# Row maxima at 0.615 instead of 0.57 steps per group of three products, in the second layer of a diffusion backbone

## The chip, the core and the metric

The kernel runs on one core of a Trainium2 chip. TensorE (PE) multiplies; VectorE (DVE), ScalarE (ACT) and GpSimd (POOL) do the rest, and SyncE (SP) issues most loads. Each engine works through its own instructions in order, and semaphores tie them together. The metric is the device time of one execution in microseconds, the median of several.

## The reference

Two layers run over 2048 latent tokens of width 1024 on a grid of 32 rows by 64 columns, with 256 context tokens ahead of them. The second layer (layer 1 in the code) is neighbourhood attention with 16 heads of 64. Cut to what matters:

```python
q, k, v, z = jnp.split(jnp.dot(h, w_in), 4, axis=-1)      # 1024 columns each, latent and context tokens
q, k = rms_norm(q, q_gain), rms_norm(k, k_gain)            # per head
s_lat = einsum(q_row, k_window) * scale + rpb              # 8 grid rows, 16 of 64 columns left by a mask
s_ctx = einsum(q_row, k_ctx) * scale                       # 256 context tokens
p = softmax(concat([s_lat, s_ctx]))
o = p_lat @ v_window + p_ctx @ v_ctx
y = jnp.dot(o * silu(z), w_out)
```

## The kernel before

Everything is float32, and products are made of three passes of rounded parts (`hi*hi + hi*lo + lo*hi`); such a group of three matmuls of 512 columns for one slice of 128 of the inner dimension is one **step**. Tokens go in tiles of 128: `NT` = 18 tiles, the first `NCT` = 2 of them context.

Layer 1 has three stages. `odd_qk` makes queries and keys and writes them to DRAM (`Q1`, `K1`, `K1t`). `odd_vz`, the stage of the change, does two things at a time:

- **The projections** of values and gates, PE's main stream. A cell (t, j) is tile t times the 512 columns j: 4 and 5 are the values, 6 and 7 the gates. A cell has 8 steps (lines L131 to L133, bank `gm`). Values go over ACT to DRAM on POOL's queue (`V1`, `V1c` for context); gates pass a tanh, a product on DVE (L1639) and four transposes (L1642, tile `tp`) to DRAM. There are 65 cells: tiles 15 to 17 first, then from 14 down to 0; the last four are the values of tiles 1 and 0. `reload` brings each tile's hidden state from DRAM (L394) and splits it into `hhi` and `hlo` (L399).
- **The row maxima**, `maxes()`. For each of 16 heads and 16 blocks of 128 queries, a "row" takes the largest score that the softmax will subtract later: a product with the 256 context keys (L1689; its maxima for two rows are one reduction, L1691) and one with a window of latent keys (L1696), to whose pieces DVE adds the bias table and takes the maximum (L1702). The queries come by a small load per four rows (`mq`, L1683) which ACT sorts into `mz`; the tables come per head (`mtab`, L1673), and POOL adds the window's mask to them (L1674, L1675). PE and DVE pass the scores through five PSUM banks `mx`. At a head's end the maxima are transposed (L1658) and go to `M1` in DRAM.

`weave` joins the two: after each projection step it adds `ratio` to what is due and issues that many rows. With `head` = 32, rows begin when four cells are done. A row may fall behind its step by `lag` = 15; past that the projections are held until it is issued, and once the rows have all been asked for, the hold tightens by the same ratio:

```python
n = len(done) - lag - 1 + int(over)
if n >= 0:
    es.enter_context(self.tc.issue_after(done[min(n, len(done) - 1)].ins))
```

The order on each engine within these bounds is laid out when the program is built, by a scheduler with a time model of its own.

`odd_attention` follows. Its loads run in one chain on SP (`load`, L113), in this order: queries of head 1 (`q11`, `q21` and their maxima from `M1`), a group of keys (`kt`), values (`ov`), two bias tables (`tab`), context keys (`kc`), queries of head 0, more keys, the context values, the mask (`maskk`), and then the next pair of heads. The first scores are those with the context keys (L1786, L1787, tile `st`). The scores with latent keys wait in `st` until DVE adds the table (L1945), to which POOL has added the mask (L1783). These tiles take over memory of the stage before: the query tile `q11` lies where the row maxima had their keys `mk`, and `maskk` lies where the last projection weights are.

Of the kernel before, what the change touches and what calls it, by code (L numbers as in the profile page):

```python
# [61 lines left out]
def rect(kind, g, c):  # L62

    (r, nr), (k, nk) = reach(kind, 0, g), reach(kind, 1, c)
    while nr * nk < 256:
        k, nk = (k, nk + 1) if k == 0 else (k - 1, nk + 1)
    return (r, nr), (k, nk)


def even(a, n):  # L70

    b = a // 2 * 2
    return b, (a + n + 1) // 2 * 2 - b, a - b


def pieces(kind, ax, g, a, n):

    blocks, u = BLOCKS[kind][ax], AXES[ax][2]
    out = []
    for p in range(n):  # L80
        i = blocks.index((g, a + p) if (g, a + p) in blocks else (1, a + p - u * (g - 1)))
        if out and out[-1][1] + out[-1][2] == i:
            out[-1][2] += 1
        else:
            out.append([p, i, 1])
    return out


class Kern:
# [1523 lines left out]
    def odd_vz(self, ws, win, hT):  # L1613
# [4 lines left out]
        with ExitStack() as es:  # L1618
# [37 lines left out]
            def row(h, mc):  # L1656
                pt = self.tl(pp, [P, 512], "mx", bufs=5)
                nc.tensor.transpose(pt[:16, :P], mc[:], self.ident[:])  # L1658
                r = self.tl(mp, [P, P], "mr", F32R, bufs=1)
                self.act(r[:16], pt[:16, :P], AF.Copy, scale=-1.0)  # L1660
                for g in range(4):
                    nc.gpsimd.dma_start(self.M1[h, g * 512 : g * 512 + 512].rearrange("(a c b) -> c a b", a=8, c=4),
                                        r[4 * g : 4 * g + 4].rearrange("c (a b) -> c a b", a=8).bitcast(F32))

            def maxes():
                for h in range(16):
                    j, b = h // 2, (h % 2) * 64
                    with self.tc.issue_after(self.wload.ins):
                        if b == 0:
                            k = self.tl(mp, [P, T], "mk", F32R, bufs=2)  # L1670
                            nc.sync.dma_start(k[:].bitcast(F32), self.K1[j])
                        tb = self.tl(mp, [P, NR, NC], "mtab", bufs=2)
                        nc.sync.dma_start(tb[:], self.i["rpb_q"][h].rearrange("p (r c) -> p r c", r=NR))  # L1673
                    nc.gpsimd.tensor_tensor(out=tb[:], in0=tb[:], in1=mk[:, :NR].unsqueeze(2).to_broadcast([P, NR, NC]), op=ALU.add)  # L1674
                    nc.gpsimd.tensor_tensor(out=tb[:], in0=tb[:], in1=mk[:, NR:].unsqueeze(1).to_broadcast([P, NR, NC]), op=ALU.add)  # L1675
                    m = self.tl(mp, [P, 16, 5], "mm")
                    nc.vector.memset(m[:], -3e38)
                    kl = k[:, CTX:].rearrange("d (r c) -> d r c", r=32)
                    for R in range(16):
                        g, c = divmod(R, 4)  # L1680
                        if c == 0:
                            q = self.tl(mp, [P, 512], "mq", F32R, bufs=1)
                            nc.sync.dma_start(q[b : b + 64].bitcast(F32), self.Q1[0, j, b : b + 64, g * 512 : g * 512 + 512])  # L1683
                            zt = zq[h % 2][g % 2]
                            self.by_tile(zt[b : b + 64], q[b : b + 64])
                        lh = zt[:, c * P : c * P + P]
                        if c % 2 == 0:
                            pc = self.tl(pp, [P, 2, CTX], "mx", bufs=5)
                        nc.tensor.matmul(pc[:, c % 2, :], lh, k[:, :CTX], start=True, stop=True)  # L1689
                        if c % 2 == 1:  # L1690
                            nc.vector.tensor_reduce(out=m[:, R - 1 : R + 1, 0], in_=pc[:], axis=AX.X, op=ALU.max)  # L1691
                        (r0, nr), (c0, w) = rect("q", g, c)
                        ps = self.tl(pp, [P, 512], "mx", bufs=5)
                        a, n, d = even(c0, w)
                        ps = ps[:, : nr * n].rearrange("p (r c) -> p r c", r=nr)
                        mm = nc.tensor.matmul(ps, lh, kl[:, r0 : r0 + nr, a : a + n], start=True, stop=True)  # L1696
                        ps = ps[:, :, d : d + w]
                        n = 1
                        for ro, ri, rn in pieces("q", 0, g, r0, nr):
                            for co, ci, cn in pieces("q", 1, c, c0, w):  # L1700
                                s = ps[:, ro : ro + rn, co : co + cn]
                                nc.vector.tensor_tensor_reduce(out=s, in0=s, in1=tb[:, ri : ri + rn, ci : ci + cn], scale=1.0,  # L1702
                                                               scalar=-3e38, op0=ALU.add, op1=ALU.max, accum_out=m[:, R, n : n + 1])
                                n += 1
                        yield mm
                        if R == 5 and h:
                            row(*turn)
                    mc = self.tl(mp, [P, 16], "mc", bufs=1)
                    nc.vector.tensor_reduce(out=mc[:], in_=m[:], axis=AX.X, op=ALU.max)
                    turn = (h, mc)  # L1710
                row(*turn)
# [1 line left out]
            first = [NT - 3, NT - 2, NT - 1]  # L1713
            cells = self.cells(first + list(range(NT - 3))[::-1], (4, 5, 6, 7), lambda t, j: (j > 4 or t < NT - 3) and (j < 6 or t >= NCT))
            gemms = self.stream(cells, hT, cell, lambda t: self.reload(1, t))
            self.weave(gemms, maxes(), 0.57, 15, 32)


    def odd_attention(self, out, right, left, wout):
# [508 lines left out]
```

## Time and profile before

| | |
|---|---|
| median of 3 runs | 3563.59 us (3560.05 to 3564.49) |
| the profiled execution | 3565.63 us, of it 3563.9 us from first to last instruction |
| busy: PE, DVE, ACT, POOL | 97%, 68%, 41%, 35% |
| the stage of the change: first row product to last projection | 2556.3 to 2985.2 us of the span |
| from the last projection to the first score product of attention | 19.55 us without PE |
| last instruction of the span | 3563.9 us |

Most times below are positions in the span. "A <- B" in a list of waits means that A waited for B; behind it stand the total in us, the number of times and the longest. A line of a timeline has start and duration in us, the engine, the source line, the operation, the tiles it writes and reads, and in brackets the idle time before it and what ended that. SPq is SP's DMA queue as its sequencer issues it.

### The profile page before, as it was taken

What the parts mean: (1) busy time and instruction counts of PE and PEld (TensorE: products, weight loads), DVE (VectorE), ACT (ScalarE), POOL (GpSimd) and SP (SyncE); (2) the same over time, 40 slices, a digit from 0 to 9 for tenths busy, and PEclk for the clock granted to TensorE, in tenths of its full rate; (3) what the DMA queues carried; (4) which work ended last, traced back from release to release, by engine and by line L of the source; (5) the groups of instructions that cost most, each with busy time, mean ns of one, the idle gap of its engine ahead of it and who ended that gap; (6) DMA issues with size and microseconds to landing.
All of it is one profiled execution on the core that took longest, in us unless ns stands there. A gap on an engine that the chain in (4) does not pass through costs nothing. (4 is left out here: it accounts for less than half of the span.)

```text
span 3563.9 us, 54063 instructions
## 1 busy us (share of the span) xinstructions
PE 3453.2 (97%) x19460; PEld 2666.8 (75%) x19460; DVE 2431.0 (68%) x4798; ACT 1449.8 (41%) x2647; POOL 1243.9 (35%) x1400
## 2 busy tenths in 40 slices
PE   7999999999999999999999999999999997999999
PEld 6888987888896666665557878888788885556577
DVE  4677756888885777768876655444477874666875
ACT  5445542111113554546664354544322222555532
POOL 1333431111111333422211144334234443888852
PEclk9999999999999999999999999999999998999999
DMA  7555555232315242334525765445744447888684
GB/s 253 144 158 157 152 141 152 91 107 93 102 65 165 62 133 80 103 116 132 176 79 142 144 193 151 134 138 164 244 139 159 155 152 183 206 223 219 192 234 79
DMA packets 379596, 526.75 MB, mean 148 GB/s; under 512 B 34633, under 2 KB 254233, under 8 KB 372882
## 3 DMA queue, kind: packets, MB, share of 16 engines
q1 hardware_dynamic: 326450, 405.32, 39.3%
q0 software_dynamic: 29856, 82.14, 9.2%
q10 hardware_dynamic: 23024, 35.85, 3.0%
q8 instruction: 154, 2.52, 0.3%
q14 instruction: 112, 0.92, 0.1%
HBM read 344.39 MB, written 196.60 MB: 152 GB/s over the span
## 5 line engine op out<-in xcount | busy, mean ns | idle before, releaser
L699 DVE TENSOR_REDUCE mm<-mx 128x1 f32<-128x512 f32 (+1 forms) x656 | 388.3, 627 | 82.5 <-PE mx L698 75.5
L108 ACT ACTIVATE apt<-st 128x1024 f32<-128x1024 f32 (+1 forms) x296 | 300.0, 1014 | 313.2 <-PE st L1168 298.0
L1175 DVE TENSOR_TENSOR acc<-acc,apt 128x1024 f32<-128x1024 f32 x256 | 340.6, 1330 | 80.6 <-ACT apt L108 61.5
L1168 PE MATMUL st<-aq,akh 64*128 64x512 f32 x1728 | 313.9, 411 | 1.1 <-ACT apt L108 0.8
L1078 PE MATMUL av<-apt,av 128*64 128x512 f32 x1152 | 265.8, 598 | 0.0
L1945 DVE TENSOR_TENSOR opt<-st,tab 128x64 f32<-128x64 f32 (+10 forms) x576 | 144.2, 315 | 151.0 <-PE st L1787 67.6
L1826 POOL TENSOR_TENSOR oacc<-oacc,opt 128x576 f32<-128x576 f32 (+5 forms) x192 | 223.3, 1186 | 39.2 <-ACT rl L108 19.6
L698 PE MATMUL mx<-mk,mq 96*128 96x512 f32 (+1 forms) x656 | 236.0, 373 | 0.5 <-DVE mm L699 0.5
L1168 PE MATMUL st<-aq,akl 64*128 64x512 f32 (+1 forms) x1152 | 231.4, 393 | 0.0
L1702 DVE CUSTOM_DVE_ANT_1 mx<-mx,mtab 128x217 f32<-128x217 f32 (+12 forms) x576 | 183.6, 339 | 53.3 <-PE mx L1696 40.6
L108 ACT ACTIVATE u<-gm 128x352 f32<-128x352 f32 (+1 forms) x140 | 68.4, 496 | 370.9 <-PE gm L133 208.5
L1168 PEld LDWEIGHTS st<-aq,akh 64*128 64x128 f32 x1728 | 154.1, 187 | 83.6 <-ACT apt L108 28.0
L1078 PEld LDWEIGHTS av<-apt,av 128*64 128x64 f32 x1152 | 76.2, 136 | 135.3 <-issue 134.3
L108 ACT ACTIVATE opt<-opt 128x930 f32<-128x930 f32 (+8 forms) x130 | 104.5, 805 | 108.6 <-DVE opt L1945 104.2
L698 PEld LDWEIGHTS mx<-mk,mq 96*128 96x128 f32 x656 | 121.2, 188 | 12.9 <-DVE mm L699 1.6
L1168 PEld LDWEIGHTS st<-aq,akl 64*128 64x128 f32 (+1 forms) x1152 | 112.6, 186 | 24.2
L1691 DVE TENSOR_REDUCE mm<-mx 128x2 f32<-128x512 f32 x128 | 88.3, 690 | 46.1 <-PE mx L1689 45.0
L220 POOL TENSOR_TENSOR oss<-oss,mhalf 128x8 f32<-128x8 f32 x68 | 113.3, 1666 | 5.0
L131 PE MATMUL gm<-w1h,hhi 128*128 128x512 f32 x280 | 112.2, 401 | 0.0
L133 PE MATMUL gm<-w1h,hlo 128*128 128x512 f32 x280 | 110.3, 394 | 0.0
L1786 PE MATMUL st<-q,kt 128*128 128x480 f32 (+5 forms) x256 | 99.5, 391 | 11.1 <-DVE opt L1945 8.1
L132 PE MATMUL gm<-w1l,hhi 128*128 128x512 f32 x280 | 110.0, 393 | 0.0
(694 smaller groups left out, 9743.9 us busy)
## 6 DMA issues: line engine op xcount, KB each, us to landing
q<-Q SPq DMA_DIRECT2D x48, 512.0 KB
H<-x ACTq DMA_DIRECT2D x32, 512.0 KB
adaw<-ada_w SPq DMA_DIRECT2D x64, 256.0 KB
wraw<-w_od SPq DMA_DIRECT2D x64, 256.0 KB
K1t<-okt POOLq DMA_DIRECT2D x32, 512.0 KB, 10.1
kt<-K1t SPq DMA_DIRECT2D x32, 512.0 KB
x<-H SPq DMA_DIRECT2D x31, 512.0 KB
mtab<-rpb_q SPq DMA_DIRECT2D x16, 899.0 KB
```

The costliest lines, as they stand in the source:

```text
L108: return self.nc.scalar.activation(out, in_, func, **kw)
L131: self.nc.tensor.matmul(out, lh(k), rh(k), start=start and j == 0, stop=False)
L133: yield self.nc.tensor.matmul(out, ll(k), rh(k), start=False, stop=stop and j == n - 1)
L220: return g.tensor_tensor(out=out, in0=out, in1=self.mhalf[:, : shp[1]], op=ALU.pow)
L698: mm = nc.tensor.matmul(ps[:, :w], q[:A_QK, (t % 6) * P : (t % 6) * P + P], k[:A_QK, k0 : k0 + w], start=True, stop=True)
L699: nc.vector.tensor_reduce(out=m[:, t, n : n + 1], in_=ps[:, :w], axis=AX.X, op=ALU.max)
L1078: mm = nc.tensor.matmul(O[j, nb][i * 64 : i * 64 + 64, :w], V[j, kt // TT][:, kt % TT, i * 64 : i * 64 + 64], pts[:, i, :w], start=n == 0, ...
L1168: mm = nc.tensor.matmul(ps[:, o // 64, :w], k[o : o + r, kb, kq], Q[o : o + r, qb, :w], start=m == 0, stop=m == 4)
L1175: added = nc.vector.tensor_tensor(out=acc[:, :, :w], in0=a[:, :, :w], in1=pts[:, :, :w], op=ALU.add)
L1702: nc.vector.tensor_tensor_reduce(out=s, in0=s, in1=tb[:, ri : ri + rn, ci : ci + cn], scale=1.0, scalar=-3e38, op0=ALU.add, op1=ALU.max, a ...
L1826: self.psum = nc.gpsimd.tensor_tensor(out=a, in0=a, in1=pts[:, :, a0 - r0 : a1 - r0, :], op=ALU.add)
L1945: bias = nc.vector.tensor_tensor(out=pt[:, d[0], d[1]], in0=ps[:, d[0], d[1]], in1=tabs[j][i][:, ri : ri + rn, ci : ci + cn], op=ALU.add)
```

## The change

One number: `ratio` in the call that weaves the stage goes from 0.57 to 0.615. Nothing is computed differently, and no instruction is added or taken away but for how rows of the same kind stand beside each other.

```diff
             gemms = self.stream(cells, hT, cell, lambda t: self.reload(1, t))
-            self.weave(gemms, maxes(), 0.57, 15, 32)
+            self.weave(gemms, maxes(), 0.615, 15, 32)
```

Two places show what moves. The first is PE where the last head's last rows stand. Before, they stand in the first half of cell (1, 5), whose bank is `gm_4836`; one more cell follows it.

```order
L132 MATMUL gm_4836_27919<-w1l_4003_23377,hhi_4785_27603 128x512
L133 MATMUL gm_4836_27919<-w1h_4002_23376,hlo_4786_27604 128x512
L1696 MATMUL mx_4817_27787<-mk_4734_27333,mz11_4051_23653 128x384
L131 MATMUL gm_4836_27919<-w1h_4002_23376,hhi_4785_27603 128x512
L132 MATMUL gm_4836_27919<-w1l_4003_23377,hhi_4785_27603 128x512
L133 MATMUL gm_4836_27919<-w1h_4002_23376,hlo_4786_27604 128x512
L131 MATMUL gm_4836_27919<-w1h_4002_23376,hhi_4785_27603 128x512
L132 MATMUL gm_4836_27919<-w1l_4003_23377,hhi_4785_27603 128x512
L133 MATMUL gm_4836_27919<-w1h_4002_23376,hlo_4786_27604 128x512
L1696 MATMUL mx_4822_27811<-mk_4734_27333,mz11_4051_23653 128x288
```

Now they stand at the seam between cells (2, 5) and (2, 6), banks `gm_4819` and `gm_4821`:

```order
L1689 MATMUL mx_4801_27645<-mk_4719_27205,mz11_4051_23653 128x256 x2
L132 MATMUL gm_4819_27755<-w1l_4003_23377,hhi_4770_27466 128x512
L133 MATMUL gm_4819_27755<-w1h_4002_23376,hlo_4771_27467 128x512
L1696 MATMUL mx_4802_27647<-mk_4719_27205,mz11_4051_23653 128x384
L131 MATMUL gm_4821_27784<-w2h_4031_23538,hhi_4770_27466 128x512
L132 MATMUL gm_4821_27784<-w2l_4032_23539,hhi_4770_27466 128x512
L133 MATMUL gm_4821_27784<-w2h_4031_23538,hlo_4771_27467 128x512
L1696 MATMUL mx_4807_27671<-mk_4719_27205,mz11_4051_23653 128x288
```

From the last L1696 on, 12 projection steps stood behind it and 47 stand there now, with two sets of gate transposes among them. Through the middle of the stage the rows lag by 15 to 17 in both programs.

The second place is SP's queue where the last small loads of the rows meet the first loads of attention. Before:

```order
L394 DMA x_4829_27857<-H 128x1024
L1683 DMA mq_4764_27503<-Q1 64x512
L1683 DMA mq_4778_27575<-Q1 64x512
L1683 DMA mq_4792_27646<-Q1 64x512
L1683 DMA mq_4803_27705<-Q1 64x512
L1683 DMA mq_4812_27756<-Q1 64x512
L113 DMA q11_4844_28038<-Q1 64x2048 x2
L113 DMA q21_4845_28039<-Q1 64x2048
```

Now:

```order
L1683 DMA mq_4753_27384<-Q1 64x512
L1683 DMA mq_4763_27441<-Q1 64x512
L1683 DMA mq_4777_27512<-Q1 64x512
L1683 DMA mq_4788_27568<-Q1 64x512
L1683 DMA mq_4797_27619<-Q1 64x512
L394 DMA x_4829_27857<-H 128x1024
L113 DMA q11_4844_28038<-Q1 64x2048 x2
L113 DMA q21_4845_28039<-Q1 64x2048
```

The reload of tile 0 (`x_4829`) now stands right ahead of the queries. The order of attention's loads is the same. By the semaphore counts in the two programs, `q11` waits for the last row's product (L1696) in both; the first keys `kt1` and the first table `tab0` have new waits, for projections of tile 2 that stand 40 and 33 steps ahead of the end; and `maskk` waits for the last projection product in both. PE's and DVE's orders differ in some places in the first pair of heads of attention and are the same behind it.

## The prediction

> **What bounds the kernel now.** I began with the page: a span of 3563.9 us with PE busy for 97% of it. The stage that is changed shows as steady in the 40 slices, so I asked for stretches of it: one in the thick of the row maxima, and then the last 33 us and the passage into attention.
>
> ```profile
> 2760.00:2880.00 120.00, 120.00 (x597) 100.81 (x596) 97.53 (x410) 31.50 (x54) 52.97 (x46) 1.00 0.49 156
> ...
> 2952.00:2964.90 12.90, 12.90 (x66) 10.72 (x65) 11.14 (x51) 5.05 (x8) 3.96 (x6) 1.00 0.11 32
> 2964.90:2976.90 12.00, 12.00 (x61) 10.19 (x60) 8.40 (x35) 1.90 (x4) 1.17 (x2) 1.00 0.33 111
> 2976.90:2985.20 8.30, 8.30 (x37) 6.40 (x35) 1.41 (x9) 0.86 (x2) 2.22 (x4) 1.00 0.84 190
> 2985.20:2995.00 9.80, 0.02 (x1) 0.00 (x0) 0.00 (x0) 0.60 (x1) 2.28 (x5) 0.67 1.12 285
> 2995.00:3004.80 9.80, 0.03 (x1) 0.06 (x1) 0.00 (x0) 0.00 (x0) 0.00 (x0) 0.50 1.05 257
> 3004.80:3014.40 9.60, 9.34 (x23) 6.92 (x24) 0.00 (x0) 4.35 (x8) 2.36 (x2) 0.50 1.05 306
> 3014.40:3025.00 10.60, 9.69 (x35) 4.44 (x35) 6.75 (x26) 2.88 (x4) 7.20 (x6) 0.61 1.03 231
> ```
>
> The columns are the stretch, then busy time of PE, weight loads, DVE, ACT and POOL, the granted clock, the DMA share and GB/s. In the stage PE has no gap (120.00 of 120.00): the projections and the rows fill it, whatever their order. After 2985.2 PE does nothing for two stretches while the DMA engines are full (1.12, 1.05), and then it works at half clock until past 3014.4. Before 2976.9 the same DMA engines stood at 0.11 and 0.33. So the passage is where the time can move. The list of waits and the PE's timeline say what it waits for.
>
> ```profile
> PE st L1786 <- DMA q<-Q: 19.6, 1, 19.6
> SPq L113 <- PE mx L1696: 17.8, 1, 17.8
> ...
> PE st L1786 <- DVE opt L1945: 2.0, 6, 0.6
> ```
>
> ```profile
> 2976.54 0.30 PE L1696 MATMUL mx<-mk,mz 128*128 128x288 f32 x1
> ...
> 2977.38 0.39 PE L131 MATMUL gm<-w1h,hhi 128*128 128x512 f32 x1
> ...
> 2982.19 0.39 PE L131 MATMUL gm<-w1h,hhi 128*128 128x512 f32 x1
> ...
> 2984.83 0.39 PE L133 MATMUL gm<-w1h,hlo 128*128 128x512 f32 x1
> 3004.77 1.62 PE L1786 MATMUL st<-q,kc 128*128 128x512 f32 x3 [19.55 <-DMA q<-Q]
> ```
>
> ```profile
> 2976.87 1.72 SPq L113 DMA_DIRECT2D q<-Q  x3
> ...
> 2980.91 10.00 SPq L113 DMA_DIRECT2D tab<-rpb_k  x2
> ...
> 2992.10 1.88 SPq L113 DMA_DIRECT2D q<-Q  x3
> 2994.83 0.26 SPq L113 DMA_DIRECT2D q<-M  x1
> ...
> 2999.81 0.54 SPq L113 DMA_DIRECT2D maskk<-maskk  x1
> ```
>
> The last row product starts at 2976.54; 0.33 us later SP, which had waited 17.8 us for it, issues the first attention loads, because the query tiles lie in memory that the rows' keys held. The projections end at 2985.22 (2984.83 + 0.39). The queries and keys that the first score product needs are there only at 3004.77, and PE loses 19.55 us. The next thing late is the mask: its load goes out at 2999.81, POOL adds it to the tables at 3012.04, and only then does DVE's first bias start.
>
> ```profile
> 3012.04 4.73 POOL L1783 TENSOR_TENSOR tab<-tab,maskk 128x1034 f32<-128x1034 f32 x2 [24.34 <-PE st L1787]
> ```
>
> ```profile
> 3014.46 1.16 DVE L1945 TENSOR_TENSOR opt<-st,tab 128x32 f32<-128x32 f32 x6 [36.02 <-POOL tab L1783]
> ```
>
> From 3014.46 on attention runs; that is 29.2 us after the projections' end. Behind it PE waits for 2.0 us in all over the next 85 us (0.6 at most, for DVE), so a shift of this point shifts the end.
>
> **The change, part by part.** No instruction is added or removed; 256 rows are dealt out over fewer projection steps. There are 65 cells of 8 steps, so 520. With 32 steps of head start, 256 rows take 256/0.57 = 449 steps before and 256/0.615 = 416 now. A row may lag 16 behind, and in the built order it does: the last row's product stands 12 steps ahead of the last projection before, 47 steps ahead now.
>
> *Steps to time.* Seven steps go from 2977.38 to 2982.19, so 0.687 us each. Behind the last row now stand 47 steps and two sets of four transposes.
>
> ```profile
> 2965.97 0.60 PE L1642 MATMUL tp<-ident,ovz 128*128 128x128 f32 x4
> 2966.32 0.48 PE L131 MATMUL gm<-w0h,hhi 128*128 128x512 f32 x1
> ```
>
> A set takes 0.35 us, so the first query load gets a lead of 47 x 0.687 + 0.7 = 33.0 us on the projections' end, in place of 8.35 us (2976.87 to 2985.22).
>
> *The loads in their new place.* SP issues in order. One reload of hidden states is now ahead of the queries, but the split that it waits for needs only the tile done 64 steps before the end, so it is gone in time. Two later loads gain waits on memory that the projections free: the first keys at 40 steps before the end (27.5 us) and the first table at 33 steps (22.7 us). What the first score product needs took 27.9 us from 2976.87 to 3004.77, which is 0.84 x 8.3 + 1.12 x 9.8 + 1.05 x 9.8 = 28.2 us of full DMA. In the 33.0 us now open, other traffic takes about 0.22 (the mean of 0.11 and 0.33), which leaves 25.9 us. The deficit is 2.3 us: I take the queries to land 2 us after the projections' end. The bounds are 0 (some of that traffic is already inside the 28.2) and 6 us (the two waits leave the queue empty for a while). So PE's wait of 19.55 us becomes about 2 us.
>
> *The mask.* Its load waits for the very last projection product in both programs, so it can't move ahead of the end. Before, it took 12.2 us from issue (2999.81) to POOL's start, in a full queue. The nearest transfer at a half-loaded queue is a table of the rows:
>
> ```profile
> 2646.24 0.34 SPq L1673 DMA_DIRECT2D mtab<-rpb_q  x1
> ```
>
> ```profile
> 2651.70 3.20 POOL L1674 TENSOR_TENSOR mtab<-mtab,maskq 128x1798 f32<-128x1798 f32 x1 [12.95 <-DMA mtab<-rpb_q]
> ```
>
> That is 5.5 us. I take 7.5 us, nearer to the lower end, because the next tables can't be issued beside it until the last value store is done, but one pair of keys is still ahead of it. With 0.5 us to issue and 2.42 us of POOL (3012.04 to 3014.46) the first bias starts 10.4 us after the end, in place of 29.2: **18.8 us earlier**, with bounds of 8.4 us (gain 20.8) and 15.1 us (gain 14.1). The mask now ends last, and the 2 us of the queries lie under it.
>
> *The faster rows.* Per PE step the rows come 0.615/0.57 = 1.079 times as fast, at most so per us. What they ask of DVE, POOL (52.97 of 120), ACT (31.50) and SP's small loads grows by that. DVE is the nearest to its end:
>
> ```profile
> DVE mm L1691 <- PE mx L1689: 9.4, 16, 1.5
> DVE mx L1702 <- PE mx L1696: 7.6, 19, 0.8
> DVE hlo L399 <- ACT hhi L108: 1.8, 1, 1.8
> ```
>
> In the densest 120 us it waits 18.8 us, so its work and its gaps take 101.2 us; 101.2 x 1.079 = 109.2 us, still under 120. Five banks of PSUM stand between PE and DVE. PE never waited for DVE here; I charge **1 us** for short meetings, between 0 and the whole lost pace: rows as slow as before and the new 47 steps behind them, 35 x 0.687 + 0.7 = 24.7 us.
>
> *The sum.* -18.8 + 1.0 = -17.8 us. The profiled execution took 3565.63 us, so 3547.8; it lies 2.04 us above the median of 3563.59, so the forecast is **3545.8 us**, 0.5% faster.
>
> **The rivals.** *1. DVE becomes the bound.* PE's row products then wait for banks. It decides from a pace 120/101.2 = 1.186 times the old one on; the change asks 1.079, and against it speak the 18.8 us of waiting; for it, that the rows' pieces differ in size, so that a run of long ones can ask more than the mean. At its worst the stage ends 24.7 us later, and attention still gains its 18.8: 3563.59 + 24.7 - 18.8 = 3569.5 us, slower than before.
>
> *2. The DMA engines bound the passage.* Stores of values and gates and the moved loads share them; if the queries land 6 us after the end and the mask takes its old 12.2 us behind them, the first bias starts at 6 + 12.2 + 2.4 = 20.6 us, a gain of 8.6 less 1.0: 3556.0 us. For it speaks that the share was above 1.0 for 50 us, against it the 0.11 and 0.33 of the tail. The Trainium skill ("Trainium Kernel Development and Optimization", Key Constraints) says that DMAs from the SP, ACT and POOL queues run on the same 16 engines and interleave; the shares of 1.05 and 1.12 over all queues agree, and by it the moved loads don't get the tail for themselves.
>
> *3. The clock stays up.* Now PE stands long enough to be cut to half clock; the shortest pause after which the trace shows that is this one:
>
> ```profile
> 2556.28 0.58 PE L1689 MATMUL mx<-mk,mz 128*128 128x256 f32 x1 [3.42 <-DMA mk<-K]
> ```
>
> ```profile
> 2555.00:2558.00 3.00, 1.72 (x6) 1.53 (x7) 0.00 (x0) 0.00 (x0) 0.00 (x0) 0.52 1.02 402
> 2558.00:2561.00 3.00, 3.00 (x9) 2.42 (x9) 0.69 (x1) 0.00 (x0) 2.38 (x1) 0.50 0.98 372
> ```
>
> After the change PE would pause 2 us for the queries, work off its scores (9.34 x 0.50 = 4.7 us at full clock) and pause again until 10.4, for 3.7 us. If neither closes the clock, the 9.69 us of PE work in 3014.4 to 3025.0, done at 0.61, shrinks by 9.69 x 0.39 = 3.8 us: 3542.0 us. I leave it out of the sum, since the second pause is a little longer than 3.42 us. The Trainium skill ("TensorE: Matmul & The Clock Gate", Part 1: The HAM clock gate) has the clock halved after an idle window of about 3.4 us, with which the pause above agrees, and restored after about 3.4 us of sustained work; the second half doesn't fit 3004.8 to 3014.4, where PE is busy for 9.34 of 9.60 us at 0.50. By the page a mask that comes half a microsecond sooner would keep the clock.
>
> **How the numbers follow.** Forecast 0.55; clock 0.15; DMA 0.17; DVE 0.13. Forecast and clock are faster by more than 0.2% (7.1 us, about what a measurement of this kernel can tell from no change). Of the DMA case 0.14 is faster and 0.03 within, since its price is near the border. Of the DVE case, whose full price is 0.17%, I put 0.07 beyond 0.2% (a PE that waits would lose clock as well) and 0.06 within. That gives 0.84, 0.09 and 0.07. The range goes from 3539.0 (the clock case with the mask at its lower bound and no wait for DVE) to 3556.5 (the DMA case), and leaves out the DVE case and the tails.
>
> **What would show it.** Right: the first query load 32 to 34 us before the last projection; the wait of the first score product down from 19.55 to under 6 us; the first bias 8 to 15 us after the projections' end; the stage from its first row to its last projection as long as before within 2 us; no wait of PE on DVE above 1 us. Wrong: waits of mx on DVE inside the stage (rival 1), a first bias later than 15 us with the DMA share above 1.0 (rival 2), a granted clock of 1.00 through the passage (rival 3), or PE waiting later in the first pair of heads for a load that was not late before.

## The result, and the profile after

The changed kernel takes 3545.79 us (median of 6 runs, 3538.15 to 3548.69), the kernel before 3564.04 us on the same chip (6 runs, 3557.59 to 3567.88). The ratio is 0.9948, with a 95% interval of 0.9933 to 0.9962: 0.5% faster, and the slowest run of the one is below the fastest of the other. The profiled execution took 3543.46 us, with a span of 3541.7 us and a mean granted clock of 0.989 (before: 3565.63, 3563.9, 0.984).

The same stretches as before, taken at the new places: the stage, its tail from the first query load on, and the passage. The columns are again the stretch, busy time of PE, weight loads, DVE, ACT and POOL, the granted clock, the DMA share and GB/s.

```profile
2560.00:2943.00 383.00, 383.00 (x1911) 322.52 (x1911) 312.55 (x1337) 102.51 (x172) 165.95 (x142) 1.00 0.48 151
2943.50:2960.00 16.50, 16.50 (x76) 13.46 (x76) 3.98 (x14) 4.40 (x7) 6.15 (x10) 1.00 1.02 224
2960.00:2970.00 10.00, 10.00 (x48) 8.23 (x47) 0.00 (x0) 1.69 (x3) 1.04 (x2) 1.00 0.74 233
2970.00:2976.80 6.80, 6.78 (x30) 5.25 (x28) 0.00 (x0) 0.60 (x1) 0.69 (x2) 1.00 1.05 308
2976.80:2988.00 11.20, 6.35 (x24) 3.75 (x24) 0.41 (x4) 4.62 (x9) 5.79 (x5) 0.95 0.96 300
2988.00:2996.00 8.00, 7.46 (x24) 3.46 (x24) 6.36 (x24) 2.77 (x4) 2.73 (x2) 0.65 0.99 209
2996.00:3010.00 14.00, 13.75 (x91) 9.32 (x89) 7.45 (x17) 7.46 (x12) 11.88 (x11) 1.00 1.08 225
```

The stage still has no gap on PE (383.00 of 383.00). What is new is the tail: in the three stretches from 2943.50 to 2976.80 PE is full and the DMA engines are at 1.02, 0.74 and 1.05. The loads that ran over an idle PE before now run under projections. PE's timeline and SP's show the ends of it, and DVE's and POOL's show the mask:

```profile
2943.20 0.29 PE L1696 MATMUL mx<-mk,mz 128*128 128x288 f32 x1
...
2976.40 0.39 PE L133 MATMUL gm<-w1h,hlo 128*128 128x512 f32 x1
2977.47 0.96 PE L1786 MATMUL st<-q,kc 128*128 128x512 f32 x3 [0.69 <-ACT ovz L108]
...
2988.39 0.66 PE L1786 MATMUL st<-q,kt 128*128 128x384 f32 x1 [4.12 <-DVE opt L1945]
```

```profile
2943.53 1.72 SPq L113 DMA_DIRECT2D q<-Q  x3
...
2978.93 0.57 SPq L113 DMA_DIRECT2D ov<-V1c  x1
2979.62 0.52 SPq L113 DMA_DIRECT2D maskk<-maskk  x1
```

```profile
2985.21 4.70 POOL L1783 TENSOR_TENSOR tab<-tab,maskk 128x1034 f32<-128x1034 f32 x2
```

```profile
2987.59 1.17 DVE L1945 TENSOR_TENSOR opt<-st,tab 128x32 f32<-128x32 f32 x6 [30.94 <-POOL tab L1783]
```

The projections end at 2976.40 + 0.39 = 2976.79. The first query load goes out 33.3 us ahead of that, in place of 8.35. PE's wait of 19.55 us for the queries is gone: the first score product starts 0.69 us after the end, and waits for ACT. The first bias starts 10.8 us after the end, in place of 29.2. A new wait has come: at 2988.39 PE had stood 4.12 us for DVE's biases, which wait for the mask, and then it works at a clock of 0.65 for 8 us.

The span is 22.2 us shorter, but not all of that is the change. In this execution the first row product starts at 2549.29, 7.0 us earlier than before (2556.28), and nothing ahead of it was changed. An account that leaves this out starts at the first row product. From there to the end of the span it is 3563.9 - 2556.28 = 1007.6 us before and 3541.7 - 2549.29 = 992.4 us now, so 15.2 us less.

### The profile page after: what moved, and what is told of

The parts are those of the page before. It is cut to its first block, busy times and chain, and to the rows that moved or that the text cites. A ratio compares the mean times of both kernels' runs of the same rounds, so it can differ in the third digit from the quotient of the medians.

```text
span 3541.7 us, 54052 instructions
## 1 busy us (share of the span) xinstructions
PE 3446.2 (97%) x19460; PEld 2665.2 (75%) x19460; DVE 2430.6 (69%) x4798; ACT 1451.3 (41%) x2647; POOL 1247.1 (35%) x1400
## 5 line engine op out<-in xcount | busy, mean ns | idle before, releaser
L1702 DVE CUSTOM_DVE_ANT_1 mx<-mx,mtab 128x217 f32<-128x217 f32 (+14 forms) x576 | 182.4, 341 | 34.1 <-PE mx L1696 25.4
L1786 PE MATMUL st<-q,kt 128*128 128x480 f32 (+5 forms) x256 | 99.0, 389 | 17.1 <-DVE opt L1945 11.7
```

## The experiments

The theory: the lead of the first query load on the projections' end sets the passage, the mask's load sets what is left of it, and the rows' faster pace costs nothing. The rivals: DVE is close to being the bound, so that the pace has a price; or part of the 18 us is an accident of the execution.

All eight kernels compute the whole reference. In the table, the lead is from the first query load to the projections' end, the stage from the first row product to that end; PE's wait is the one ahead of the first score product; "from the first row" is from there to the end of the span, in the one profiled execution. Times are medians of 5 runs or more (3 for the kernel before), with their ratio to the kernel before on the same chip (medians 3563.8 us beside e1 to e4, 3562.7 beside e5 to e8).

| kernel | lead | stage | PE's wait | first bias after the end | from the first row | time | ratio (95%) |
|---|---|---|---|---|---|---|---|
| before | 8.35 | 428.9 | 19.55 | 29.2 | 1007.6 | 3563.6 | |
| changed, 0.615 | 33.3 | 427.5 | 0.69 | 10.8 | 992.4 | 3545.8 | 0.9948 (0.9933 to 0.9962) |
| e5, the same again | 33.3 | 428.0 | 0.69 + 0.93 | 12.9 | 993.9 | 3543.6 | 0.9948 (0.9936 to 0.9961) |
| e1, 0.57, lag 0 | 27.1 | 437.3 | 6.48 | 16.8 | 1000.8 | 3559.1 | 0.9989 (0.998 to 0.9998) |
| e2, 0.59 | 19.8 | 432.8 | 10.84 | 20.6 | 1003.9 | 3557.0 | 0.9981 (0.9972 to 0.999) |
| e3, 0.75 | 90.8 | 430.9 | 0.69 | 7.2 | 985.9 | 3544.7 | 0.9947 (0.9933 to 0.9961) |
| e4, 0.615, mask early | 33.3 | 426.8 | 0.69 | 5.9 | 986.5 | 3542.8 | 0.9945 (0.9933 to 0.9957) |
| e6, 0.75, mask early | 95.1 | 434.4 | 0.69 | 5.1 | 993.2 | 3547.8 | 0.9959 (0.9947 to 0.9972) |
| e7, 1.0 | 157.4 | 459.9 | 0.69 | 7.5 | 1021.2 | 3575.9 | 1.0034 (1.0021 to 1.0047) |
| e8, e4, next values later | 33.3 | 426.9 | 0.69 | 6.5 | 980.7 | 3542.1 | 0.994 (0.9927 to 0.9952) |

**e1: the lead without the pace.** The rows keep 0.57 and may lag by none in place of 15.

```
-            self.weave(gemms, maxes(), 0.57, 15, 32)
+            self.weave(gemms, maxes(), 0.57, 0, 32)
```

> The pace stays at 0.57, but a row may lag by 1 instead of 16, so the last row's product stands 38 steps ahead of the last projection (12 before, 47 in the changed kernel). My theory, that only the lead of the first query load counts: lead 38 x 0.687 + 0.7 = 26.8 us, queries there 0 to 4 us after the projections' end, first bias 11 to 14 us after it, 15 to 18 us faster than before: 3546 to 3549 us on a median of 3564. The rival that the pace itself saves time inside the stage: no gain, 3562 to 3566 us. Against both, the tighter lag may make PE wait for DVE in the stage: each us of that is added.

It took 3559.1 us, 10 us above the range that the theory gave. Some of PE's waits, from the head of the stage into the passage:

```profile
PE st L1786 <- DMA q<-Q: 6.5, 1, 6.5
PE mx L1696 <- DVE mm L1702: 3.7, 2, 3.0
...
PE tp L1642 <- ACT ozt L108: 1.8, 1, 1.8
PE mx L1689 <- DVE mm L1702: 1.0, 1, 1.0
```

```profile
2964.95 1.72 SPq L113 DMA_DIRECT2D q<-Q  x3
2967.20 11.16 SPq L113 DMA_DIRECT2D kt<-K1t  x2
```

The lead does what the theory says: the first bias comes 12.5 us sooner after the end at the old ratio. But 6.5 us are still lost to the queries, more than expected, and SP needs 11.16 us to issue the two key loads right behind them. The stage is 8.4 us longer: with no lag PE waits 4.7 us on DVE and 1.8 us on ACT in it, which it did not before; what makes up the rest, no view names. So the lead works without the faster pace, but without the lag the stage takes back more than half of what it gives: from the first row on 6.8 us are left.

**e2: a smaller step.** The same line with 0.59, lag 15.

> Ratio 0.59: 28 steps behind the last row, a lead of 28 x 0.687 + 0.35 = 19.6 us. Lead theory: the loads, which took 27.9 us, are there 8 to 11 us after the projections' end, the first bias comes 17 to 20 us after it, 9 to 12 us faster than before: 3552 to 3555 us. If the passage were bound by something that the lead does not move, the time would stand at that of before; if any lead sufficed, at that of the changed kernel, 3546.

It took 3557.0 us, 2 us above the expected range. PE's wait for the queries is 10.84 us and the first bias comes at 20.6 us, both between the two kernels. The stage is 3.9 us longer than before, and one wait in it is not explained by the theory:

```profile
PE st L1786 <- DMA q<-Q: 10.8, 1, 10.8
...
PE mx L1696 <- DVE mm L1691: 3.5, 1, 3.5
```

PE waits 3.5 us for DVE once, at a slower pace than the changed kernel's, which has no such wait. So a meeting with DVE does not go by the mean pace alone; whether the order of the rows or chance made this one, a single profile can't tell.

**e3: a much larger step.** The same line with 0.75, where the prediction's reckoning (1.186 times the old pace at most) has DVE past its end.

> Ratio 0.75, 126 steps behind the last row. This is where the DVE rival decides: the rows' part of the stage would take 341 x 0.687 + 256 x 0.29 = 308 us of PE and by DVE's share of 101.2 in 120 us some 322 us or more. The theory of a DVE bound beyond 1.186 times the pace: PE waits for DVE for 10 to 25 us in the stage, the passage gains the same 18 us as at 0.615, in all 3556 to 3571 us. If DVE has more room than its waits show: no waits, 3545 to 3547 us, as at 0.615.

It took 3544.7 us, as was expected if DVE had more room than its waits show: no bound. Two stretches of its stage, and some of PE's waits from shortly ahead of it on:

```profile
2720.00:2760.00 40.00, 40.00 (x203) 33.84 (x202) 36.87 (x174) 10.61 (x19) 22.91 (x20) 1.00 0.57 178
2840.00:2880.00 40.00, 39.73 (x202) 33.67 (x202) 37.29 (x177) 11.08 (x19) 22.80 (x19) 1.00 0.49 153
```

```profile
PE gm L131 <- ACT ovz L108: 3.4, 2, 1.8
...
PE mx L1696 <- DVE mm L1702: 0.3, 1, 0.3
PE mx L1696 <- DVE mm L1691: 0.2, 1, 0.2
```

DVE is busy for 37.29 of 40 us, and PE's row products wait on it for 0.5 us in the whole stage. The rows run from 2557.08 to 2895.93, 338.9 us in place of 420.3: 1.24 times the old pace.

**e4: the mask early.** On the changed kernel, the mask is also loaded into a buffer of values that is still free, ahead of the tables' first use, and added from there.

```
             Q[0, 0] = query(0, 0)
+            m0 = self.tl(vp[1], [P, NT, P], "ov", bufs=1)[:].rearrange("p t d -> p (t d)")[:, : NR * NC]
+            self.load(m0, self.i["maskk"])
+            m0 = m0.rearrange("p (r c) -> p r c", r=NR)
+            for tb in tabs[0]:
+                nc.gpsimd.tensor_tensor(out=tb[:], in0=tb[:], in1=m0, op=ALU.add)
...
-            mask(tabs[0])
```

> The changed kernel (0.615), but the mask for the first pair of heads is loaded a first time, behind the queries, into a tile of values that is not in use yet and whose memory only the rows held, so POOL can add it without waiting for the last projection. Theory that the mask ends last in the passage: first bias 3 to 7 us after the projections' end instead of 10.8, PE's pause of 4.1 us and the half clock behind it (some 8 us long) gone, 5 to 9 us faster than the changed kernel: 3537 to 3541 us. Rival, that the DMA engines bound what follows: the pause comes back later for another load, 3544 to 3547 us.

It took 3542.8 us, between the two expectations. DVE and POOL show the mask in its new place, the stretches the clock:

```profile
2986.29 4.78 POOL L1883 TENSOR_TENSOR tab<-tab,ov 128x1034 f32<-128x1034 f32 x2 [1.93 <-DMA ov<-maskk]
```

```profile
2988.76 0.65 DVE L1949 TENSOR_TENSOR opt<-st,tab 128x32 f32<-128x32 f32 x4 [26.00 <-POOL tab L1883]
```

```profile
2982.90:2990.00 7.10, 5.97 (x24) 3.93 (x25) 0.89 (x6) 4.62 (x9) 4.25 (x3) 1.00 1.00 318
2990.00:3000.00 10.00, 9.74 (x52) 4.95 (x51) 5.97 (x22) 4.56 (x8) 7.01 (x6) 1.00 0.91 245
...
3010.00:3020.00 10.00, 6.95 (x56) 4.44 (x56) 3.96 (x10) 3.86 (x5) 10.00 (x9) 0.94 1.10 252
```

```profile
PE st L1786 <- DMA kt<-K1t: 5.6, 1, 5.6
```

The first bias is at 5.9 us after the end instead of 10.8, the clock stays at 1.00 through the passage, and 34 us behind the projections' end PE begins to wait 5.6 us for the last group of the first pair's keys. So the mask was what ended last, as predicted, and behind it the keys are next.

**e5: the changed kernel again**, to see how much of the first profile is an accident.

> The changed kernel once more. Its profile began the stage 7.0 us earlier than that of before, though nothing that stands ahead of the stage has changed. If that is chance between executions: the first row product within 3 us of 2556, and from there to the projections' end 427 to 430 us, the first bias 9 to 12 us behind it; time 3543 to 3549 us. If the change had a hand in it, 2549 again.

Its first row product starts at 2556.83, where the kernel before has 2556.28 and the first profile of the change 2549.29. So the 7.0 us ahead of the stage were an accident of that execution; over all ten profiles this product starts between 2549.29 and 2561.89. The lead is 33.3 us again, and PE's passage has the same waits, a little otherwise:

```profile
2985.51 0.96 PE L1786 MATMUL st<-q,kc 128*128 128x512 f32 x3 [0.69 <-ACT ovz L108]
2988.11 1.22 PE L1787 MATMUL st<-q,kc 65*128 65x512 f32 x2 [0.93 <-DMA q<-Q]
...
2998.49 0.66 PE L1786 MATMUL st<-q,kt 128*128 128x384 f32 x1 [2.88 <-DVE opt L1945]
```

The first bias, 12.9 us after the end, is 0.9 us later than expected. Its five runs give a ratio of 0.9948 again; the profiled one was the slowest of them (3552.47 us).

**e6: 0.75 and the early mask together.**

> Ratio 0.75 with the early mask. With a lead of some 90 us all first loads are there; the only thing left for the passage is POOL's addition of the mask, which needs no load any more. Theory that the loads' late start is all there is to the passage: first bias 3 to 5 us after the projections' end instead of 7.2, no half clock, 3539 to 3542 us. Rival, that the keys held up in SP's queue behind the values of the next pair give it back, as in the early-mask run at 0.615: 3542 to 3546 us.

It took 3547.8 us, above both expectations and no better than either alone:

```profile
PE gm L131 <- ACT ovz L108: 5.7, 2, 4.4
...
PE st L1786 <- DMA kt<-K1t: 5.5, 1, 5.5
```

The stage is 6.9 us longer than the changed kernel's: 4.4 us are the longer of the projections' two waits on ACT (the other stands ahead of the first row), and 2.3 us are lost to a lower clock. The wait for the keys is there again.

**e7: where DVE does become the bound.** The same line with 1.0.

> Ratio 1.0, to see DVE as the bound, which it was not at 0.75. The rows then stand among 268 projection steps, 268 x 0.687 + 256 x 0.29 = 258 us of PE, while DVE was busy for 298 us in the 340 us of the rows' part at 0.75. DVE bound: PE waits for DVE for 40 to 60 us in the stage, less the passage's gain of 22 us: 3580 to 3605 us. No DVE bound: 3543 to 3548 us.

It took 3575.9 us, 0.34% slower than the kernel before, and 4 us below what was expected of a DVE bound. The stretch of its rows, and two of PE's waits in it:

```profile
2555.00:2860.00 305.00, 287.62 (x1421) 237.38 (x1420) 274.44 (x1337) 82.53 (x139) 164.11 (x124) 0.98 0.53 165
```

```profile
PE mx L1696 <- DVE mm L1691: 6.7, 7, 1.0
PE mx L1689 <- DVE mm L1702: 3.5, 2, 3.2
```

PE has 17.4 us of gaps in these 305 us. Waits for DVE are 15.2 of them, in 25 pieces of at most 3.2 us, where 40 to 60 us were expected. The stage is 31 us longer than before: 20 us are idle time and 3 us lost clock, and the other 8 us no view names. The rows take 302.2 us where the ratio asked for 258. So 1.39 times the old pace is all that they reach, and the point from which DVE decides lies between 1.24 and 1.39.

**e8: e4, with the second pair's values asked for later**: in SP's queue they now stand behind the first pair's last group of keys and the second pair's context keys.

```
-                        elif (kind, n) == ("l", 6):
+                        elif (kind, n) == ("l", 9 if j == 0 else 6):
+                            if j == 0:
+                                kc[j + 1] = keys(j + 1, 0, CTX, kcp, "kc")
                             V[j + 1] = values(j + 1)
                             values_ctx(j + 1, V[j + 1])
```

> The early-mask kernel at 0.615, and in the first pair of heads the values of the next pair are asked for behind the last group of keys and the context keys instead of ahead of them. Theory that PE's wait of 5.6 us for keys comes from their place behind the values in SP's queue: that wait gone, 3536 to 3540 us. Rival, that the DMA engines as a whole are behind (their share stood at 1.04 to 1.10): the wait stays or moves, 3541 to 3545 us.

```profile
3014.93 1.08 SPq L113 DMA_DIRECT2D kt<-K1t  x2
3016.19 1.12 SPq L113 DMA_DIRECT2D kc<-K1t  x2
3017.40 0.54 SPq L113 DMA_DIRECT2D ov<-V  x1
```

In e4 the key loads were issued at 3013.77, behind a values load that took 9.43 us to issue; here they go ahead of it, and the wait of 5.6 us in that place is gone. So that wait did come from the keys' place in the queue. The time does not show it clearly: 3542.1 us is the lowest median of all, but 2 us above what the theory gave, and e4 and the changed kernel lie within the scatter of its runs (3537.57 to 3548.29). From the first row on its profiled execution is 11.7 us shorter than the changed kernel's first; its median is 3.7 us below that kernel's, and 1.5 us below that of e5, which ran on the same chip.

## Why the prediction was right, step by step

The forecast of 3545.8 us was met to 0.1 us. That is luck, closer than its steps deserve: two errors in the mask's term cancelled, a part was lost again behind the passage, and medians of 5 or 6 runs that spread over 10 us or more don't settle single microseconds.

*The lead* was right: 33.3 us for 33.0 (47 steps and two sets of transposes). The 12 and 47 steps were read from the built order; to come near them from the ratio, the lag of 16 has to be counted in rows, which are 28 steps at 0.57 and 26 at 0.615: 520 - 32 - 449 - 28 = 11 and 520 - 32 - 416 - 26 = 46. Over the kernels with lag 15, a lead of 8.35, 19.8 and 33.3 us leaves a wait of 19.55, 10.84 and 0.69 us.

*The queries* were taken to land 2 us after the end. (33.0 us less 22% are 25.7, not 25.9, which changes little.) Those of the first score product were there by 0.7 us after the end in both executions; in e5 a later one waited 0.93 us for more of them, until 3.3 us after it. Both lie between the bounds of 0 and 6 us. The upper bound supposed a queue that stands empty for a while; the tail's DMA shares of 1.02, 0.74 and 1.05 show an almost full one.

*The mask* came out as forecast, 10.8 us (12.9 in e5) for 10.4, by two wrong terms. Its load was to go out 0.5 us after the end; it went out at 2979.62, 2.83 us after, since SP stood before it at the context values' load (2978.93), which waited for values to be stored. From issue to POOL's start it was to take 7.5 us and took 5.6 (2979.62 to 2985.21), as the table of the rows had (5.5). POOL's share was 2.38 for 2.42.

*DVE* was charged 1 us and cost nothing: the stage is 1.4 us shorter in the changed kernel and 0.9 in e5, and no row product waits for DVE in it. The failed step here is rival 1's condition. It took DVE's work and its unnamed gaps (101.2 of 120 us) as fixed, and put the deciding point at 1.186 times the old pace; its busy time alone, 97.53 of 120, would have put it at 1.230. But e3 at 1.24 shows no bound, and e7 reached 1.39. The rows' parts of the kernel before and of e3 show why:

```profile
2560.00:2980.00 420.00, 420.00 (x2075) 352.73 (x2074) 318.01 (x1354) 110.36 (x184) 177.99 (x150) 1.00 0.47 148
```

```profile
2560.00:2900.00 340.00, 339.41 (x1706) 286.16 (x1706) 297.69 (x1345) 93.78 (x158) 171.27 (x134) 1.00 0.51 162
```

For the same 256 rows DVE is busy for 318.01 us before, 297.69 in e3 and 274.44 in e7. Part of that, about 40, 36 and 30 us, is work for the projections (L399, L1639), of which fewer stand among faster rows. The rest falls too, so the time that the records give to one row shrinks when more is asked, and not only the gaps between. Why it does was not measured.

*The clock* was left out of the sum at nothing, since PE would pause 3.7 us; it paused 4.12 us, and the clock stood at 0.65 over the 8 us behind. But its price changed all the same, and differs between executions of one kernel. To see it, stretches of 2.5 us from the projections' end to the end of the span were summed: idle is their length less PE's busy time, lost clock is PE's busy time times (1 - granted clock).

| kernel | first 50 us: idle, lost clock | all behind them: idle, lost clock | end to end of span |
|---|---|---|---|
| before | 20.7, 8.4 | 24.7, 8.1 | 578.7 |
| changed | 6.0, 2.5 | 27.3, 13.0 | 564.9 |
| e5, the same | 5.5, 6.6 | 25.9, 11.4 | 565.9 |
| e1 | 8.9, 7.4 | 23.2, 6.2 | 563.5 |
| e2 | 12.0, 8.3 | 24.8, 9.2 | 571.1 |
| e3 | 4.6, 1.6 | 23.7, 7.6 | 555.0 |
| e4 | 8.2, 2.8 | 24.3, 5.1 | 559.7 |
| e6 | 7.0, 3.3 | 23.4, 7.9 | 558.8 |
| e7 | 5.1, 4.8 | 26.2, 7.0 | 561.3 |
| e8 | 2.4, 1.6 | 23.3, 7.9 | 553.8 |

What is left when idle time and lost clock are taken off is 516.1 to 519.3 us in all ten, so the account holds what differs. In the passage the change gains 29.1 - 8.5 = 20.6 us in its first execution and 29.1 - 12.1 = 17.0 in e5, on either side of the 18.8 forecast. Some 15 us of each are idle time, the rest is clock.

*The end.* That a shift of the first bias shifts the end was only nearly right. Behind the first 50 us the two executions lose 7.5 and 4.5 us more than the kernel before, so that the end comes 13.8 and 12.8 us sooner, counted from the projections' end. The prediction named a later wait as a sign and gave it no price. Of what was given back, 4.9 and 3.3 us are lost clock and 2.6 and 1.2 us idle time. Waits for keys account for about as much idle time; those from 3010 to 3340 of the changed kernel, then of e5, then of the kernel before:

```profile
PE st L1786 <- DMA kt<-K1t: 2.5, 2, 1.6
PE st L1787 <- DMA kt<-K1t: 1.3, 2, 0.7
```

```profile
PE st L1787 <- DMA kt<-K1t: 0.9, 1, 0.9
...
PE st L1786 <- DMA kt<-K1t: 0.5, 1, 0.5
```

```profile
PE st L1787 <- DMA kt<-K1t: 0.4, 1, 0.4
```

That is 3.4 and 1.0 us more. e3, e4 and e8 reach or undercut the 32.8 us of the kernel before in this part, with a passage no later than the change's. So the loss does not follow from an early passage as such. It stands in the middle of attention: from 80 to 320 us behind the projections' end the kernel before and e1, e2, e3, e4, e6 and e8 lose 6.0 to 6.7 us, none of it to the clock, and the changed kernel's two executions lose 13.1 and 10.4, of it 3.3 and 1.7 lost clock (e7: 9.6 and 1.7). That both of them do, and seven other kernels do not, speaks for this order of loads. The medians, 18.2 and 19.1 us below those of the kernel before where the two executions gain 15.2 and 13.7 from the first row on, speak for chance. Which it is stays open.

*Rivals.* DVE as the bound is refuted at 0.615 and 0.75 and shown at 1.0. The DMA engines were nearly full at the passage here too (0.96, 0.99 and 1.08 behind the projections' end), but with a lead of 33 us they no longer held the first bias up; e2, with its 20.6 us for the first bias and 3557.0 us, is what rival 2 would have looked like. The clock that stays up is e4: 1.00 through the passage, and 4.9 us won in the first bias. The keys' wait of 5.6 us took that back: by the ratios, 0.9945 and 0.9948, e4 is 1 us faster than the changed kernel, which is within the noise.

## What to carry to other kernels

When loads of the next stage wait for memory that side work holds, finish the side work earlier and look at what it was hidden under: here 25 us more of lead turned 19 us of an idle main engine into loads under matmuls. Take what a profile says of a side engine's free time as a lower bound, since its gaps and even its busy time for the same work can shrink under load: at 1.24 times the pace DVE still held nothing up, where the waits had said 1.186 and the busy column 1.230. And price the next late load too: each time one wait went (queries, mask), the next one in the same queue (mask, keys) took its place.

## What the runs showed of the hardware

*A load can hold SP for ten microseconds.* Most loads take 0.3 to 2 us to issue here. A few, right behind several others, took about ten, and all that is queued behind them waits, the keys at 3008.34 among them:

```profile
2996.83 0.38 SPq L113 DMA_DIRECT2D ov<-V  x1
2997.25 10.99 SPq L113 DMA_DIRECT2D ov<-V1c  x1
3008.34 1.26 SPq L113 DMA_DIRECT2D kt<-K1t  x2
```

The 10.00 us of two table loads before and the 9.43 us in e4 stand right behind an `ov<-V` load too; the 11.16 us of two key loads in e1 stand behind queries alone. Two table loads 3.66 us after an `ov<-V` load took 3.99 us. What the long ones share is that much was issued just ahead; how much it takes was not measured.

*The clock is not set by the longest pause alone.* In e5 PE's longest pauses at the head of the passage were 0.69 and 0.93 us, and its clock fell before the long one and stayed down until past 3004:

```profile
2985.50:2992.00 6.50, 5.30 (x14) 3.48 (x15) 0.00 (x0) 2.86 (x6) 0.54 (x1) 0.69 1.04 320
2992.00:2996.00 4.00, 3.61 (x12) 2.81 (x10) 0.00 (x0) 1.49 (x3) 3.19 (x3) 0.50 0.77 257
...
3000.00:3004.00 4.00, 3.85 (x11) 1.77 (x12) 4.00 (x19) 2.12 (x4) 0.00 (x0) 0.50 0.97 202
```

The first profile of the same kernel shows 0.95 there. The Trainium skill ("TensorE: Matmul & The Clock Gate", Part 1: The HAM clock gate) says that the window in which activity is watched runs freely, so that the point of change differs between runs; two executions of one program with different clocks agree with that. It also has the clock restored after about 3.4 us of sustained work. Taken by itself that doesn't fit: PE worked at 0.50 without a pause for 6.0 us in e5 (2989.59 to 2995.61) and for 6.0 us in the kernel before (3008.96 to 3014.98). With a window that runs freely, 6.0 us of work need not hold a whole one (an estimate from the Trainium skill's 3.4 us: only 6.8 us must), so the prediction's "doesn't fit" is more than these runs show.

*DVE busy for 37.29 of 40 us does not hold PE up.* In e3 PE has gaps of 0.27 us beside that. From 2800 to 2840 in e7 DVE was busy for 37.38 us, hardly more, and PE has gaps of 2.00 us; every wait of PE that the profile names there is for DVE. So the share alone doesn't tell; that the rows' demand comes in bursts is a guess, which was not measured.
